# Expert weights in a two-layer MoE trunk: the limit on loads in flight is lifted, the room for them alone holds them back

## Chip, cores and metric

One core of one Trainium2 chip. Times are device microseconds of one execution. Before the change: 1047.03 us, median of three runs.

## What is computed

A trunk of two decoder layers over 512 tokens of width 1024, in float32. Layer 0 mixes tokens by RWKV-7 and gated linear attention, layer 1 by sparse attention. Each layer ends with the same kind of mixture of experts, which is what the change touches:

```
def _moe(h, router_w, router_bias, w_gate, w_up, w_down):
    s = jax.nn.sigmoid(hf @ router_w)
    ...                              # best of 4 groups of 4 experts, best 2 experts in it
    y = jnp.zeros(hf.shape, f32)
    for e in range(N_EXPERTS):       # 16
        he = (jax.nn.silu(hf @ w_gate[e]) * (hf @ w_up[e])) @ w_down[e]
        y = y + comb[:, e:e + 1] * he
    return y

h = _layer_norm(DN_ALPHA * x + mix, ln1_g[l], ln1_b[l])
ffn = _moe(h, ...)
x = _layer_norm(DN_ALPHA * h + ffn, ln2_g[l], ln2_b[l])
```

Gate and up are 1024 x 256 for each expert, down is 256 x 1024: 3.15 MB of float32 weights per expert, 50 MB per layer, and each is used once.

## The kernel before

Each layer is a mixer and then `moe_ln`. By the time of `moe_ln` the tokens' rows are stored in device memory as hD, and a copy of the residual as Y. `moe_ln` takes the 16 experts in order. A list of at most 128 tokens has been made for each expert (rtgt); what does not fit is left to a branch, `further`, which is not taken here, but where SP waits for all its DMAs to land.

For each expert the work is spread as follows. POOL issues a gather of the expert's rows, `fetch` (L974, `xg<-hD,rtgt`), two experts ahead. `turn` transposes them on PE (xtp, L986) and splits them into a high and a low part (xgh, xgl). `gate_up` loads four chunks of wgu, 128 x 1024 each, and multiplies; `hid_t` transposes the hidden values (htp, L1014); `down` loads two chunks of wdn, multiplies, copies the result to ys on ACT (L1035), and POOL issues a scatter (L1039, `Y<-ys,rtgt`) that adds it to Y. The last two experts add theirs on PE instead (zt, L1087), after Y has been read back (L1077, `hy<-Y`). There are two ys buffers. All scatters go to Y, so each one waits for the landing of the one before. In the order of one round the gate_up of expert e+1 comes before the down of expert e.

A weight chunk is loaded by SP (`Weights.part`, L566, 512 KB a load) into a raw buffer (named wr, room or hy after where its memory is), then ACT makes the rounded high part wh (L573) and DVE, or POOL for one chunk of an expert, the low part wl (L574). PE multiplies three times: high by high, low by high, high by low. The raw buffers of each layer's experts are a ring of 27, so a load may be issued when the chunk 27 loads earlier has been split. The two kinds of split outputs have nine pairs of buffers.

Two DMA queues carry all this: q1 holds what SP issues (loads, and the stores of hD and Y), q0 the gathers and scatters of POOL. Each works on all 16 DMA engines.

`Weights` is made in both layers with `flight` set to 3: a load also waits until the load three before it in program order has landed, whether or not there is room. The order of instructions on each engine is set by the scheduler of the framework; the loads stand in SP's queue in program order and are issued ahead of use as far as the ring and the limit allow, during the mixer for the first experts. The framework also gives SP's DMAs eight semaphore lanes in turn (DMAHW0 to DMAHW7); a DMA waits for the one before it in its own lane.

Of the kernel before, what the change touches and what calls it, by code (L numbers as in the profile page):

```python
# [66 lines left out]
def mm3(nc, out, ah, al, bh, bl, start, stop):  # L67
    nc.tensor.matmul(out, ah, bh, start=start, stop=False)  # L68
    nc.tensor.matmul(out, ah, bl, start=False, stop=False)  # L69
    return nc.tensor.matmul(out, al, bh, start=False, stop=stop)  # L70
# [890 lines left out]
def moe_ln(tc, k, I, L, w, xgp, xgs, tail, dbg):  # L961
# [3 lines left out]
    with ExitStack() as es:  # L965
# [5 lines left out]
        def fetch(e):  # L971

            xg = xgs[e % 3]
            nc.gpsimd.indirect_dma_start(out=xg, out_offset=None, in_=k.hD,  # L974
                                         in_offset=bass.IndirectOffsetOnAxis(ap=tgt[:, e:e + 1], axis=0),
                                         bounds_check=T - 1, oob_is_err=False)

        def turn(e):
            xg = xgs[e % 3]
            xh = xp.tile([P, KC, P], F32R, name="xgh", tag="xgh")  # L980
            xl = xp.tile([P, KC, P], F32R, name="xgl", tag="xgl")
            for hf in range(2):
                tp = k.ps.tile([P, 4, P], F32, name="xtp", tag="sm", bufs=3)
                for c in range(4):
                    cc = hf * 4 + c
                    nc.tensor.transpose(tp[:, c], xg[:, cc * P:(cc + 1) * P], k.ident)  # L986
                split_hi_lo(nc, xh[:, hf * 4:hf * 4 + 4], xl[:, hf * 4:hf * 4 + 4], tp)
            X[e] = xh, xl

        def chunk(e, j):  # L990
            return w.get(I["wgu"][L, e, :, j * 1024:(j + 1) * 1024], lo=nc.gpsimd if (j in LO0 if e == 0 else j == (1 if e > 13 else 3)) else None,
                         late=k.late if e < 2 else ())

        def gate_up(e):
            xh, xl = X.pop(e)
            gu = k.ps.tile([P, 512], F32, name="gu", tag="pj", bufs=2)
            for j in range(4):
                wh, wl = chunk(e, j)
                for c2 in range(2):
                    c = 2 * j + c2  # L1000
                    cs = slice(c2 * 512, c2 * 512 + 512)
                    mm3(nc, gu, xh[:, c], xl[:, c], wh[:, cs], wl[:, cs], c == 0, c == KC - 1)
            sg = hp.tile([P, 256], F32, name="sg", tag="sg")
            nc.scalar.activation(sg, gu[:, 0:256], AF.Sigmoid)
            tt(sg, gu[:, 0:256], sg, op=ALU.mult)
            hh = hp.tile([P, 256], F32, name="hh", tag="hh")
            stt(hh, sg, gate[:, e:e + 1], gu[:, 256:512], op0=ALU.mult, op1=ALU.mult)  # L1007
            H[e] = hh

        def hid_t(e):  # L1010
            hh = H.pop(e)
            tp = k.ps.tile([P, 2, P], F32, name="htp", tag="sm", bufs=3)
            for f in range(2):
                nc.tensor.transpose(tp[:, f], hh[:, f * P:(f + 1) * P], k.ident)  # L1014
            hth = hp.tile([P, 2, P], F32R, name="hth", tag="hth")
            htl = hp.tile([P, 2, P], F32R, name="htl", tag="htl")
            split_hi_lo(nc, hth, htl, tp)
            H[e] = hth, htl

        def down(e):  # L1020
            hth, htl = H.pop(e)
            wd = [w.get(I["wdn"][L, e, f], late=k.late if e < 2 else ()) for f in range(2)]
            if e >= 14:
                ys = w.pair()
            else:
                ys = yp.tile([P, D], F32, name="ys", tag="ys")
            for hf in range(2):
                cs = slice(hf * 512, hf * 512 + 512)
                yo = k.ps.tile([P, 512], F32, name="yo", tag="sv", bufs=2)
                for f in range(2):  # L1030
                    k.down = mm3(nc, yo, hth[:, f], htl[:, f], wd[f][0][:, cs], wd[f][1][:, cs], f == 0, f == 1)
                if e >= 14:
                    split_hi_lo(nc, ys[0][:, cs], ys[1][:, cs], yo)
                else:
                    nc.scalar.copy(ys[:, cs], yo)  # L1035
            if e >= 14:
                Y.append(ys)
                return
            nc.gpsimd.indirect_dma_start(out=k.Y, out_offset=bass.IndirectOffsetOnAxis(ap=tgt[:, e:e + 1], axis=0),  # L1039
                                         in_=ys, in_offset=None, bounds_check=T - 1, oob_is_err=False, compute_op=ALU.add)  # L1040
# [16 lines left out]
        for j, o in enumerate(onehot):  # L1057
            tt(o, k.iota[:, None, :].to_broadcast([P, NT, P]), dl[:, :, j:j + 1].to_broadcast([P, NT, P]), op=ALU.is_equal)
        gate_up(0)
        for e in range(16):  # L1060
            hid_t(e)
            if e + 2 < 16:
                fetch(e + 2)
                turn(e + 2)
            if e + 1 < 16:
                gate_up(e + 1)
            down(e)
# [328 lines left out]
def trunk(tc, ctx, k, I, out, dp, dbg):  # L1396
    nc = tc.nc
    with ExitStack() as es:
# [67 lines left out]
        with ExitStack() as ex:  # L1466
            with ExitStack() as e1:
# [46 lines left out]
                low = pool("wrawb", NRAW[1], elow)  # L1514
                w.rings(raws + [(low, NRAW[1])] + [k.h[:, i] for i in HSLOT[0]])
                moe_ln(tc, k, I, 0, w, xgp, xgs, lambda: elow.close() or x1_split(nc, k, lambda: pool("x1t", NT, ex)), dbg)
            if dbg:
                dbg("x1", k.h)
# [15 lines left out]
        with ExitStack() as e1:  # L1534
            right = lambda name, n: (pool(name, n, e1, side="right"), n)
            raws = [(few, 3)] + k.room + [right("wraw2", NRAW[2])]
            xgp = pool("xg1_", 1, e1, side="right")
            xgs = gather_bufs(xgp)
            for xg in xgs:
                nc.gpsimd.memset(xg, 0.0)  # L1540
            spl = right("wspl2", NSPL[1])[0]
            raws += [k.h[:, i] for i in HSLOT[1]] + [right("wraw3", NRAW[3]), right("wraw4", NRAW[4])]
            w = Weights(tc, raws, spl, FLIGHT)
            moe_ln(tc, k, I, 1, w, xgp, xgs, lambda: lambda i, x, cs=slice(0, D): nc.sync.dma_start(out[i * P:(i + 1) * P, cs], x[:, cs]), dbg)
# [109 lines left out]
```

## Time and profile before

| | before |
|---|---|
| median of three runs (lowest to highest) | 1047.03 us (1045.19 to 1048.56) |
| profiled execution | 1046.58 us |
| its span on the core | 1044.8 us |
| PE busy | 927.2 us, 89% |
| DVE busy | 781.9 us, 75% |
| ACT busy | 563.2 us, 54% |
| POOL busy | 318.0 us, 30% |
| q1 (SP's DMAs) | 158.02 MB, 45.2% of 16 engines |
| q0 (gathers, scatters) | 15.68 MB, 6.4% of 16 engines |

The experts of layer 0 run from about 425 to 600 us and those of layer 1 from about 855 to 1019 us of the span. Shares over the whole span mix these stages with the mixers, so the rows further down are taken from windows within them.

### The profile page before, as it was taken

What the parts mean: (1) busy time and instruction counts of PE and PEld (TensorE: products, weight loads), DVE (VectorE), ACT (ScalarE), POOL (GpSimd) and SP (SyncE); (2) the same over time, 40 slices, a digit from 0 to 9 for tenths busy, and PEclk for the clock granted to TensorE, in tenths of its full rate; (3) what the DMA queues carried; (4) which work ended last, traced back from release to release, by engine and by line L of the source; (5) the groups of instructions that cost most, each with busy time, mean ns of one, the idle gap of its engine ahead of it and who ended that gap; (6) DMA issues with size and microseconds to landing.
All of it is one profiled execution on the core that took longest, in us unless ns stands there. A gap on an engine that the chain in (4) does not pass through costs nothing. (4 is left out here: it accounts for less than half of the span.)

```text
span 1044.8 us, 14269 instructions
## 1 busy us (share of the span) xinstructions
PE 927.2 (89%) x4780; PEld 706.0 (68%) x4780; DVE 781.9 (75%) x1680; ACT 563.2 (54%) x912; POOL 318.0 (30%) x237
## 2 busy tenths in 40 slices
PE   7799988999998994899988689798999949999995
PEld 5577766776877783677776458675567737777773
DVE  4636689486587557799966678499993579989887
ACT  6435464334254213589867525154664238888872
POOL 2200212012021013375554131302400235665632
PEclk9999999999999997799999979898999959999998
DMA  6223103112106387798888745201414669889973
GB/s 222 94 66 100 51 1 91 36 57 67 35 6 228 120 284 262 256 285 271 261 268 262 250 170 161 82 1 61 141 41 165 238 215 306 281 276 301 285 248 144
DMA packets 72564, 174.72 MB, mean 167 GB/s; under 512 B 24595, under 2 KB 25907, under 8 KB 72480
## 3 DMA queue, kind: packets, MB, share of 16 engines
q1 hardware_dynamic: 63840, 158.02, 45.2%
q0 software_dynamic: 8640, 15.68, 6.4%
q8 instruction: 41, 0.67, 0.3%
q14 instruction: 43, 0.35, 0.1%
HBM read 163.23 MB, written 26.21 MB: 181 GB/s over the span
## 5 line engine op out<-in xcount | busy, mean ns | idle before, releaser
L574 DVE TENSOR_TENSOR wl<-wr,wh 128x1024 fp32r<-128x1024 f32 (+1 forms) x193 | 225.8, 1188 | 50.5 <-ACT wh L573 48.8
L573 ACT CAST wh<-wr 128x1024 fp32r<-128x1024 f32 (+2 forms) x233 | 219.4, 954 | 78.0 <-PE pj L69 29.8
L574 POOL TENSOR_TENSOR wl<-wr,wh 128x1024 fp32r<-128x1024 f32 (+2 forms) x40 | 103.5, 2592 | 167.5 <-ACT wh L573 103.7
L69 PE MATMUL gu<-wl,xgh 128*128 128x512 f32 x256 | 103.6, 405 | 0.9 <-DVE wl L574 0.8
L68 PE MATMUL gu<-wh,xgh 128*128 128x512 f32 x256 | 102.8, 402 | 0.0
L70 PE MATMUL gu<-wh,xgl 128*128 128x512 f32 x256 | 102.6, 401 | 0.0
L68 PE MATMUL pj<-xh,wh 128*128 128x512 f32 x208 | 86.2, 414 | 7.3 <-ACT xh L63 6.1
L70 PE MATMUL pj<-xh,wl 128*128 128x512 f32 x208 | 86.1, 414 | 0.0
L69 PE MATMUL pj<-xl,wh 128*128 128x512 f32 x208 | 85.6, 412 | 0.0
L1039 POOL DMA_INDIRECT Y<-ys,rtgt x28 | 58.5, 2091 | 62.9 <-ACT ys L1035 31.3
L974 POOL DMA_INDIRECT xg<-hD,rtgt x32 | 49.6, 1551 | 34.4 <-PE xtp L986 20.2
L69 PEld LDWEIGHTS gu<-wl,xgh 128*128 128x128 f32 x256 | 49.1, 192 | 14.2 <-POOL wl L574 2.4
L68 PEld LDWEIGHTS gu<-wh,xgh 128*128 128x128 f32 x256 | 49.1, 192 | 10.5 <-ACT xgh L63 0.6
L70 PEld LDWEIGHTS gu<-wh,xgl 128*128 128x128 f32 x256 | 49.0, 191 | 9.2
L69 PE MATMUL yo<-wl,hth 128*128 128x512 f32 x128 | 52.5, 410 | 2.5 <-DVE wl L574 2.4
L64 DVE TENSOR_TENSOR xgl<-xtp,xgh 128x512 fp32r<-128x512 f32 x64 | 41.1, 681 | 17.1 <-ACT xgh L63 12.3
L68 PE MATMUL yo<-wh,hth 128*128 128x512 f32 x128 | 50.8, 397 | 1.8 <-ACT hth L63 1.6
L68 PEld LDWEIGHTS pj<-xh,wh 128*128 128x128 f32 x208 | 39.8, 192 | 17.9 <-ACT xh L63 6.1
L70 PE MATMUL yo<-wh,htl 128*128 128x512 f32 x128 | 50.3, 393 | 0.0
L70 PE MATMUL pq<-wh,tl 128*128 128x512 f32 (+2 forms) x128 | 47.5, 371 | 0.0
L986 PE MATMUL xtp<-c_ident,xg 128*128 128x128 f32 x256 | 37.7, 296 | 10.7 <-DVEq L1045 5.7
L68 PE MATMUL pq<-wh,th 128*128 128x512 f32 (+2 forms) x128 | 46.6, 364 | 0.0
(422 smaller groups left out, 2215.0 us busy)
## 6 DMA issues: line engine op xcount, KB each, us to landing
wr<-in_wgu_dram SPq DMA_DIRECT2D x102, 512.0 KB, 6.5
wr<-in_wdn_dram SPq DMA_DIRECT2D x50, 512.0 KB, 7.2
wr<-in_w_dram SPq DMA_DIRECT2D x52, 256.0 KB, 2.7
wr<-in_wo_dram SPq DMA_DIRECT2D x16, 512.0 KB, 3.8
hy<-in_wgu_dram SPq DMA_DIRECT2D x15, 512.0 KB, 5.1
room<-in_wgu_dram SPq DMA_DIRECT2D x11, 512.0 KB
hy<-in_wdn_dram SPq DMA_DIRECT2D x9, 512.0 KB
hD<-hy SPq DMA_DIRECT2D x8, 512.0 KB, 2.7
```

What stands on the lines that cost most here:

```text
L64: nc.vector.tensor_tensor(lo, src, hi.bitcast(F32), op=ALU.subtract))
L68: nc.tensor.matmul(out, ah, bh, start=start, stop=False)
L69: nc.tensor.matmul(out, ah, bl, start=False, stop=False)
L70: return nc.tensor.matmul(out, al, bh, start=False, stop=stop)
L573: nc.scalar.copy(h[:, s], r[:, s])
L574: (lo or nc.vector).tensor_tensor(l[:, s], r[:, s], h[:, s].bitcast(F32), op=ALU.subtract)
L974: nc.gpsimd.indirect_dma_start(out=xg, out_offset=None, in_=k.hD, in_offset=bass.IndirectOffsetOnAxis(ap=tgt[:, e:e + 1], axis=0), bounds_ ...
L986: nc.tensor.transpose(tp[:, c], xg[:, cc * P:(cc + 1) * P], k.ident)
L1039: nc.gpsimd.indirect_dma_start(out=k.Y, out_offset=bass.IndirectOffsetOnAxis(ap=tgt[:, e:e + 1], axis=0), in_=ys, in_offset=None, bounds_c ...
```

## The change

After `gate_up(0)`, so after the program has written the loads of the first expert's four wgu chunks, `flight` is set to None. `part` then adds no wait to any later load of that layer: the first expert's wdn and all of experts 1 to 15. It happens in both layers. The object of a layer's experts is used for nothing behind them.

```
         gate_up(0)
+
+        w.flight = None
         for e in range(16):
             hid_t(e)
```

The lines that it acts on are these of `part`:

```
ld = nc.sync.dma_start(r[:, s], src[:, s])
if self.flight and len(self.loads) >= self.flight:
    behind(self.tc, ld, self.loads[-self.flight], wait=True)
```

On PE, DVE, ACT and POOL the order of instructions is the same. On SP the order is the same but for one load, and nearly every expert load has another wait. The first place is SP in the middle of layer 0's experts, six loads in a row (each row ends with the semaphores waited for: DMAHW is a lane of SP's DMAs, DVE, Activation and Pool the split that frees the raw buffer). Before:

```order
L566 DMA wr<-in_wgu_dram 128x1024 [waits DMAHW6_49,DVE_49]
L566 DMA wr<-in_wgu_dram 128x1024 [waits DMAHW7_49,DVE_49]
L566 DMA wr<-in_wgu_dram 128x1024 [waits DMAHW0_49,DVE_49]
L566 DMA wr<-in_wgu_dram 128x1024 [waits DMAHW1_49,DVE_49]
L566 DMA wr<-in_wdn_dram 128x1024 [waits DMAHW2_49,DVE_49]
L566 DMA wr<-in_wdn_dram 128x1024 [waits DMAHW3_49,DVE_49]
```

Each of these waits for the lane of the load three before it. The same six rows of SP in the changed kernel:

```order
L566 DMA wr<-in_wgu_dram 128x1024 [waits DMAHW1_49,DVE_49]
L566 DMA wr<-in_wgu_dram 128x1024 [waits DMAHW2_49,DVE_49]
L566 DMA wr<-in_wgu_dram 128x1024 [waits DMAHW3_49,DVE_49]
L566 DMA wr<-in_wgu_dram 128x1024 [waits DMAHW4_49,DVE_49]
L566 DMA wr<-in_wdn_dram 128x1024 [waits DMAHW5_49,DVE_49]
L566 DMA wr<-in_wdn_dram 128x1024 [waits DMAHW6_49,DVE_49]
```

The lane is now three further on, each load's own: it waits for the DMA eight before it, and for the room as before.

The second place is SP ahead of layer 1's experts, where the last rows of hD and Y are stored (the gathers read hD). Before:

```order
L566 DMA wr_9740<-in_wgu_dram 128x1024 [waits DMAHW2_49,PE_49]
L683 DMA hD_1387<-hy_64 128x1024 [waits Pool_49]
L683 DMA Y_1388<-hy_64 128x1024
L566 DMA hy_64<-in_wdn_dram 128x1024 [waits DMAHW4_49,DMAHW5_49,DMAHW0_49,DVE_49]
L683 DMA hD_1387<-hy_64 128x1024 [waits Pool_49]
L1650 BRANCH_PREFETCH_HINT
L683 DMA Y_1388<-hy_64 128x1024
L566 DMA wr_9752<-in_wgu_dram 128x1024 [waits DMAHW6_49,DMAHW1_49,PE_49]
L566 DMA hy_64<-in_wdn_dram 128x1024 [waits DMAHW7_49,DMAHW0_49,PE_49]
```

Here the load wr_9752 stands behind both pairs of stores. The same rows of SP in the changed kernel:

```order
L566 DMA wr_9740<-in_wgu_dram 128x1024 [waits DMAHW3_49,PE_49]
L566 DMA wr_9752<-in_wgu_dram 128x1024 [waits DMAHW4_49,PE_49]
L683 DMA hD_1387<-hy_64 128x1024 [waits DMAHW5_49,Pool_49]
L683 DMA Y_1388<-hy_64 128x1024
L566 DMA hy_64<-in_wdn_dram 128x1024 [waits DMAHW6_49,DMAHW5_49,DVE_49]
L683 DMA hD_1387<-hy_64 128x1024 [waits DMAHW0_49,Pool_49]
L1652 BRANCH_PREFETCH_HINT
L683 DMA Y_1388<-hy_64 128x1024 [waits DMAHW1_49]
L566 DMA hy_64<-in_wdn_dram 128x1024 [waits DMAHW1_49,DMAHW2_49,DMAHW0_49,PE_49]
```

The load wr_9752, which waits for PE to leave its buffer, has moved ahead of both pairs of stores, and the stores wait for lanes.

## Rows read from the trace of the kernel before

**Rows 1.** The page: its span, and one DMA queue (packets, MB, share of engines).

```profile
span 1044.8 us, 14269 instructions
...
q0 software_dynamic: 8640, 15.68, 6.4%
```

**Rows 2.** Windows: length, busy us (instructions) per engine, PE clock, DMA share, GB/s.

```profile
480.00:500.00 20.00, 19.52 (x96) 15.81 (x95) 18.31 (x22) 17.92 (x26) 13.28 (x7) 1.00 0.87 274
...
980.00:1000.00 20.00, 19.49 (x94) 15.16 (x93) 18.10 (x20) 17.43 (x25) 11.09 (x5) 1.00 0.89 283
```

**Rows 3.** SP's waits, 425 to 620, then 845 to 1030: total, times, longest.

```profile
SPq L566 <- DMA wr<-in_wgu_dram: 67.5, 37, 4.9
SPq L566 <- DMA wr<-in_wdn_dram: 35.1, 18, 5.4
...
SPq L566 <- POOL wl L574: 7.7, 3, 4.8
...
SPq L566 <- DMA wr<-in_wgu_dram: 63.0, 33, 4.8
```

**Rows 4.** ACT's waits from 425 to 620 us.

```profile
ACT wh L573 <- DMA wr<-in_wgu_dram: 12.7, 10, 3.8
```

**Rows 5.** Timeline of PE, layer 0: start, length, instruction, idle before and its releaser.

```profile
464.01 0.41 PE L1014 MATMUL htp<-c_ident,hh 128*128 128x128 f32 x2 [0.17 <-DVE hh L1007]
...
532.50 0.41 PE L1014 MATMUL htp<-c_ident,hh 128*128 128x128 f32 x2 [0.30 <-DVE hh L1007]
...
590.66 0.38 PE L1014 MATMUL htp<-c_ident,hh 128*128 128x128 f32 x2
```

**Rows 6.** Timeline of POOL, in layer 0 and from 925 in layer 1.

```profile
477.10 1.59 POOL L1039 DMA_INDIRECT Y<-ys,rtgt  x1 [1.60 <-ACT wh L573]
...
485.50 2.39 POOL L1039 DMA_INDIRECT Y<-ys,rtgt  x1 [0.16 <-ACT xgh L63]
...
492.69 2.38 POOL L574 TENSOR_TENSOR wl<-wr,wh 128x1024 fp32r<-128x1024 f32 x1 [2.69 <-issue]
...
585.30 1.93 POOL L1039 DMA_INDIRECT Y<-ys,rtgt  x1 [3.30 <-ACT hth L63]
...
925.25 2.27 POOL L1039 DMA_INDIRECT Y<-ys,rtgt  x1 [3.54 <-ACT ys L1035]
927.00 2.96 POOL L574 TENSOR_TENSOR wl<-wr,wh 128x1024 fp32r<-128x1024 f32 x1
...
935.51 2.27 POOL L1039 DMA_INDIRECT Y<-ys,rtgt  x1 [3.53 <-ACT ys L1035]
```

**Rows 7.** Issue to landing: scatters of 440-540, 860-980, at 477; gathers at 422, 426.

```profile
Y<-ys,rtgt POOLq DMA_INDIRECT x10, 9.2
...
Y<-ys,rtgt POOLq DMA_INDIRECT x11, 8.8
...
DMA to landing us min/median/max: 7.6/7.6/7.6
...
xg<-hD,rtgt POOLq DMA_INDIRECT x1, 4.3
...
xg<-hD,rtgt POOLq DMA_INDIRECT x1, 8.8
```

**Rows 8.** The page's costliest groups: busy, mean ns, idle before and its main releaser.

```profile
L69 PEld LDWEIGHTS gu<-wl,xgh 128*128 128x128 f32 x256 | 49.1, 192 | 14.2 <-POOL wl L574 2.4
```

**Rows 9.** Timelines of SP and, last row, PE at the end of layer 0's experts.

```profile
578.47 6.61 SPq L566 DMA_DIRECT2D wr<-in_wdn_dram  x4
...
596.58 1.75 SPq L1077 DMA_DIRECT2D hy<-Y  x4
...
600.00 2.05 PE L1087 MATMUL zt<-hy,c_ident 128*128 128x512 f32 x2 [4.36 <-DMA hy<-Y]
```

**Rows 10.** Timeline of SP ahead of layer 1's experts.

```profile
840.91 0.32 SPq L683 DMA_DIRECT2D hD<-hy  x1
...
842.76 0.38 SPq L566 DMA_DIRECT2D wr<-in_wgu_dram  x1
```

More of the change, by code (lines that the diff above doesn't have):

```diff
@@ L1059, in moe_ln @@
         gate_up(0)
+        w.flight = None
         for e in range(16):
```

## The prediction

> **What bounds the kernel now.** I read the page first, for the share of the span that each engine is busy and for the two DMA queues, then the windows of the two expert stages, then what SP, ACT and PE waited for there, and last the timelines of POOL and PE. The profiled execution has a span of 1044.8 us [rows 1] and took 1046.58 us, 0.45 under the median of 1047.03; the sum below is made against 1046.58. The change touches only the two expert stages, about 425 to 600 us (layer 0) and 855 to 1019 us (layer 1), and the loads that are issued ahead of them.
>
> In both stages PE is busy nearly all the time (19.5 of 20 us) and the DMA engines nearly so: share 0.87 at 274 GB/s in layer 0, 0.89 at 283 in layer 1 [rows 2]. SP spends most of its time on the limit that the change lifts. In layer 0 the waits of a load for an earlier load come to 67.5 + 35.1 us for the two largest kinds (126.9 with two smaller ones); waits for room are 7.7 us in one row. Layer 1 has 63.0 in its largest row [rows 3]. So the limit does bind, for half of each stage. Does anybody wait for the weights that come later because of it? In layer 0 yes, towards the end: ACT's cast of a fresh weight waits 12.7 us for loads of wgu [rows 4]. The rounds show it: the first transposes of two experts seven rounds apart stand at 464.01 and 532.50, so 9.78 us a round, and the next five rounds reach 590.66, 11.63 a round [rows 5]. Those five cost 58.16 − 5 x 9.78 = **9.2 us** too much. In layer 1 nobody waits for a weight: its rounds are 10.26 us from the first to the last full one, as the starts of the scatters at 925.25 and 935.51 show [rows 6], and among ACT's waits there the loads are next to nothing. What holds layer 1's round is another thing. POOL adds each expert's result to Y by a scatter, one after the other since all go to Y. A scatter lands 8.8 us (median) after its issue in layer 1 and 9.2 in layer 0 [rows 7], and the next is issued 0.8 us after that: the one issued at 477.10 landed after 7.6 us, at 484.7, and the next started at 485.50 [rows 6, 7]. A scatter and its 0.8 are 9.6 to 10 us: **as long as a round, in both layers**. In layer 1 the split of the last wgu chunk (wl, 927.00) stands right behind the scatter on POOL, and PE waits for it a little now (2.4 us over the kernel, [rows 8]); in layer 0 POOL does the scatter, the gather and then wl, with 2.69 us idle before wl [rows 6].
>
> **The change, part by part.** (1) The wait goes away, from every load of experts 1 to 15 in both layers; no instruction is added. What remains is the room (27 raw buffers) and the eight semaphore lanes over which SP's DMAs rotate: each load now waits for the DMA eight before it in place of the load three before it. So the limit is eight, not none.
>
> (2) The load queue fills. Six loads of 0.524 MB make 3.15 MB per expert; queue q0 moved 15.68 MB in about 30 gather and scatter pairs [rows 1], 0.52 MB each. A round needs 3.67 MB. By the windows a fully busy DMA moves 274/0.87 = 315 to 283/0.89 = 318 GB/s [rows 2], so a round is **11.6 us of DMA work**, against 9.78 and 10.26 of round. The limit of three hides this today: loads fall behind PE's use and eat the lead that they won before the stage. Without it SP has a backlog of up to eight loads until all weights are in, and the scatter and the gather must share the engines with it.
>
> (3) What the scatter then takes is not in the trace. Bounds: 7.6 us (the shortest one, less than now) and, if it stands behind five more loads of 0.524 MB/316 GB/s = 1.66 us, 8.8 + 8.3 = 17.1 us. The nearest rows: the gather issued at 422.74 with one load ahead landed in 4.3 us and one at 426.52 with three ahead in 8.8 [rows 7]; the scatter at 585.30 [rows 6], with the last of four loads and two vectors of 512 KB just ahead of it, was done for SP's next step at 596.58, 11.3 us later [rows 9]. So it grows with what SP has queued before it, by 1 to 2 us per transfer. I take it that it grows until the chain of scatters holds the rounds at the DMA's own 11.6 us, where the backlog stops growing (landing 10.8).
>
> By the Trainium skill, "DMA: Bandwidth & Descriptors", section "Queues, rings and completion order", each DMA engine takes turns between the queues that have work, a packet at a time; by that a deep queue of SP's would hold a scatter back no more than three loads do, which is the first rival below (1033.7 instead of 1056). The rows 7 and 9, where it took longer with more ahead, speak for order of arrival.
>
> (4) **Layer 1.** Room is for 27 loads, 4.5 rounds, so the last weight is loaded some 4 rounds before the end, and the backlog needs two or three rounds to build: 9 rounds at 11.6 − 10.26 = 1.34 give **+12.1**. Nothing is won against it: no weight was late.
>
> (5) **Layer 0.** 9 rounds at 11.6 − 9.78 = 1.82 give +16.4. Here a scatter may lag: POOL's idle 2.69 us a round and the second ys buffer let it fall behind between 2.7 us and a round of 9.8; I take 6, nearer the middle, so +10.4. The late weights of the last rounds come in time: −9.2. At the end PE waits 4.36 us for Y's rows, which wait for the last scatter [rows 9]; with no loads ahead of it, it lands in 7.6 and not 11.3: −3.7. Together **−2.5** (from −12.9, no delay, to +16.4, all of it and nothing won).
>
> (6) In layer 1 one load (the second wr load behind the two into hy) moves ahead of the last two stores of hD on SP's queue. Its buffer was free by 842.76, the last store of hD was issued at 840.91 [rows 10]: if PE frees it as late as that, stores and gathers come 1.9 us later, and behind its own 1.7 us of transfer at most 3.6 later. It may be free long before: I take 0. The waits on the limit ahead of the stages are few and lie beside the mixers' work: 0, between −1 and +2.
>
> **Sum:** 1046.58 + 12.1 − 2.5 = 1056.2; with the 0.45 to the median **1056.6 us**, 0.9% slower. Within this case the lag in layer 0 (2.7 to 9.8 us) and the count of rounds (7 to 11) give 1049 to 1068.
>
> **Rivals.** *Faster:* the scatter is not held back by a longer queue. Then layer 1 stays as it is and layer 0 gains 9.2 + 3.7 = 12.9: 1033.7 (1034.1 at the median). For it: 13% of the DMA's time in layer 0 is idle, 21 us of 160, and the landings now spread from 7.6 to 11.3 [rows 7, 9] without stopping PE in the middle; against it, [rows 7, 9] and a chain that is as long as the round already. It decides where landing plus 0.8 stays under 10.26. *Much slower:* the DMA's 0.87 is its ceiling with scatters in it, loads come no sooner, but the scatter stands behind them; then nothing is won in layer 0 and both layers stretch in full: 16.4 + 12.1 = +28.5, 1075. Against it: a share of 0.87 leaves 13% of the time in which the engines move no packet of either queue [rows 2], and a longer queue should fill it. *No change:* the chain absorbs a growing landing by its idle time and the late weights of layer 0 are paid for by layer 1, or a limit of eight acts as that of three did: 1047.
>
> **How the numbers follow.** Forecast (1049 to 1068, slower) 0.57; faster 0.24; no change 0.09; much slower 0.10. A difference under 0.3%, 3 us, could not be told from none. Faster 0.24, same 0.10 (0.01 from the forecast's lower end), slower 0.66. The range runs from 1033, the faster rival with half of what lies beyond it left out, to 1075. The forecast's own range is 1049 to 1068.
>
> **What would show it.** Right: SP's waits of loads for loads fall to a quarter, and waits for room and lanes take their place; median landing of scatters 10 to 12 us; layer 1's rounds near 11.6 through the middle and 9 to 10 in the last four; ACT's waits for wgu in layer 0 gone; DMA share over 0.95 until some 40 us before the end of each stage, then low. Wrong: landings at 9 us with the DMA at 0.95 and layer 1's rounds at 10.26 (the faster rival), or layer 0's last rounds still at 11 to 13 us with loads that are late (the slowest).

## The result: faster, and the profile after

The changed kernel took 1035.72 us (median of 16 runs, 1022.28 to 1049.77), the kernel before 1044.99 us (median of 16) in the same comparison: 9.3 us **faster** by the medians, a ratio of 0.991, where the forecast was 0.9% slower. The ratios with 95% intervals, here 0.9865 (0.9836 to 0.9894) or 14 us, leave out every run that is over 1.5% above the fastest of its kernel, here 8 of the 16 of the changed kernel and 1 of the 16 of the kernel before, so the gain is told as 9 to 14 us. A second comparison gave 0.991 (0.987 to 0.995), and 3.2 us, 0.997, by the medians of all its runs. The profiled execution took 1033.8 us with a span of 1032.0 (before: 1046.58 and 1044.8, [rows 1]). Single executions spread over 27 us (changed) and 16 us (before), so the stages are compared below, over several traces, not the spans of two.

Two windows of the expert stages of the changed kernel, with the columns of [rows 2]:

```profile
480.00:500.00 20.00, 19.51 (x96) 15.80 (x95) 18.31 (x21) 17.93 (x26) 11.77 (x7) 1.00 0.97 339
...
880.00:900.00 20.00, 18.97 (x91) 14.55 (x89) 17.78 (x21) 16.86 (x24) 12.37 (x6) 1.00 1.01 346
```

The DMA engines are full now: share 0.97 and 1.01, with 339 and 346 GB/s where [rows 2] had 0.87 at 274 and 0.89 at 283. (A packet counts in the window in which it starts, so a share can pass 1.) PE is as busy as before: 19.51 us against 19.52 in layer 0, and 18.97 in layer 1, where the kernel before has 18.98 from 900 to 920 us. So in these windows nothing was lost. SP's waits, 425 to 620 us, in the changed kernel:

```profile
SPq L566 <- DMA wr<-in_wgu_dram: 28.6, 18, 3.3
...
SPq L566 <- DVE wl L574: 19.6, 20, 2.3
SPq L566 <- POOL wl L574: 17.0, 8, 3.3
SPq L566 <- DMA wr<-in_wdn_dram: 16.0, 10, 3.2
```

The waits of loads for loads, 126.9 us before [rows 3], are 52.3 now with two smaller rows (these are the eight lanes), and the room, DVE's and POOL's wl, holds loads back for 36.6. ACT has no wait for an expert's weight left in layer 0. PE's timeline there, first transposes of experts:

```profile
498.10 0.41 PE L1014 MATMUL htp<-c_ident,hh 128*128 128x128 f32 x2 [0.31 <-DVE hh L1007]
...
527.40 0.41 PE L1014 MATMUL htp<-c_ident,hh 128*128 128x128 f32 x2 [0.19 <-DVE hh L1007]
...
538.29 0.41 PE L1014 MATMUL htp<-c_ident,hh 128*128 128x128 f32 x2 [1.24 <-DVE hh L1007]
...
584.67 0.38 PE L1014 MATMUL htp<-c_ident,hh 128*128 128x128 f32 x2
```

Three rounds from 498.10 to 527.40 are 9.77 us each, as before [rows 5]; one of 10.89 follows; and the five from 538.29 to 584.67 are 9.28 each where the last five before took 11.63. And the term on which the forecast rested, issue to landing of the scatters (minimum, median, maximum) from 480 to 550 us and from 900 to 965 in the changed kernel. The view knows the landings of three of the seven scatters in the first stretch and of three of the six in the second:

```profile
DMA to landing us min/median/max: 9.0/9.2/9.3
...
DMA to landing us min/median/max: 9.4/9.6/9.8
```

When each scatter is paired with the landings of its own semaphore in the trace, all seven have a median of 9.2 us (9.0 to 10.1) and all six one of 9.5 (9.2 to 9.8). In layer 0 this is the 9.2 of [rows 7], in layer 1 it is 0.7 above 8.8, with seven or eight loads outstanding in place of three. The loads from 480 to 550 us, paired in the same way, took 13.7 to 17.7 us, median 15.6 (36 loads), where they took 7.4 before (30 loads). When one of the seven scatters landed, two to four loads that had been issued ahead of it were still under way. **So a scatter lands before loads that were queued before it.** That settles the point on which forecast and faster rival parted. By the Trainium skill, "DMA: Bandwidth & Descriptors", section "Queues, rings and completion order", each DMA engine takes turns between the queues that have work; the trace agrees, with 9.2 us for the scatter beside 15.6 for the loads around it.

The end of layer 0's experts, PE in the changed kernel, against [rows 9]:

```profile
590.79 1.10 PE L1089 MATMUL zt<-hy,c_ident 128*128 128x512 f32 x2 [1.13 <-DMA hy<-Y]
```

PE waits 1.13 us there for Y's rows, not 4.36. And two such matmuls take 1.10 us, not 2.05. The windows just behind, of the changed kernel and then of the kernel before, show why (granted clock third from the right):

```profile
591.00:596.00 5.00, 5.00 (x18) 3.08 (x18) 2.13 (x6) 0.90 (x2) 0.00 (x0) 1.00 0.96 372
```

```profile
600.00:605.00 5.00, 5.00 (x9) 2.80 (x9) 0.70 (x1) 0.00 (x0) 0.00 (x0) 0.50 1.02 409
```

After its long wait PE ran at 0.50, 1.2 GHz, before the change: 9 instructions in 5 us. Now it stays at 1.00, 2.4 GHz: 18.

### The profile page after: what moved, and what is told of

Same layout as the page of the kernel before. It is cut to its first block, busy times and chain, and to the rows that moved or that the text cites. A ratio compares the mean times of both kernels' runs of the same rounds, so it can differ in the third digit from the quotient of the medians.

```text
span 1032.0 us, 14251 instructions
## 1 busy us (share of the span) xinstructions
PE 920.4 (89%) x4780; PEld 702.4 (68%) x4780; DVE 789.3 (76%) x1680; ACT 564.7 (55%) x912; POOL 315.9 (31%) x237
## 4 chain that ended last, share of the span: by engine, by line
PE 45%; DVE 32%; DMA 11%; issue 6%; ACT 5%; POOL 1%; DVEq 0%; SPq 0%; POOLq 0%; ACTq 0%
DVE wl L574 9%; PE pj L69 3%; PE pj L68 3%; PE pj L70 3%; DMA wr<-in_wgu_dram 3%; PE po L70 3%; PE po L69 2%; ACT wh L573 2%; DVE room L1319 2%; PE po L68 2%; DVE m L1318 2%; DMA Y<-ys,rtgt 2%; DMA xg<-hD,rtgt 2%; PE zt L1089 2%; PE gu L70 2%
## 5 line engine op out<-in xcount | busy, mean ns | idle before, releaser
L574 DVE TENSOR_TENSOR wl<-wr,wh 128x1024 fp32r<-128x1024 f32 (+1 forms) x193 | 232.9, 1226 | 37.6 <-ACT wh L573 36.1
L574 POOL TENSOR_TENSOR wl<-wr,wh 128x1024 fp32r<-128x1024 f32 (+2 forms) x40 | 105.8, 2650 | 133.7 <-ACT wh L573 57.5
L1039 POOL DMA_INDIRECT Y<-ys,rtgt x28 | 55.8, 1994 | 90.7 <-ACT ys L1035 25.2
L64 DVE TENSOR_TENSOR xgl<-xtp,xgh 128x512 fp32r<-128x512 f32 x64 | 41.3, 680 | 17.7 <-ACT xgh L63 16.4
L68 PEld LDWEIGHTS pj<-xh,wh 128*128 128x128 f32 x208 | 39.9, 192 | 17.9 <-ACT xh L63 6.3
```

Of the source, the lines that this page charges most:

```text
L64: nc.vector.tensor_tensor(lo, src, hi.bitcast(F32), op=ALU.subtract))
L574: (lo or nc.vector).tensor_tensor(l[:, s], r[:, s], h[:, s].bitcast(F32), op=ALU.subtract)
```

## The experiments

Each kernel has one trace here, and all times of stages below are worked out from these: "rounds" is the sum of the 15 gaps between the first transposes (htp) of the 16 experts, "end" the time from the last of these in layer 0 to the first transposes of the next layer (x1tp), which holds the read-back of Y and the layer norm.

| kernel | limit, layer 0 / 1 | rounds, layer 0 | end, layer 0 | rounds, layer 1 |
|---|---|---|---|---|
| before | 3 / 3 | 154.4 | 25.5 | 147.5 |
| before, again (e8) | 3 / 3 | 149.3 | 25.2 | 147.5 |
| e2 | 3 / none | 148.3 | 23.5 | 147.9 |
| changed | none / none | 143.8 | 16.9 | 147.7 |
| changed, again (e11) | none / none | 142.1 | 16.2 | 147.9 |
| e1 | none / 3 | 148.8 | 18.0 | 147.5 |
| e3 | 5 / 5 | 148.4 | 18.0 | 147.6 |
| e4 | 2 / 2 | 176.9 | 20.7 | 182.8 |
| e5, no scatters | none / none | 142.2 | 18.0 | 147.4 |
| e6 | 3, none from expert 4 on | 152.1 | 18.0 | 147.9 |
| e7, wl on DVE, experts 1 to 13 | none / none | 144.7 | 15.5 | 143.2 |
| e9, wl on DVE, all | none / none | 138.5 | 24.6 | 139.2 |
| e10, wl on DVE, all | 3 / 3 | 152.2 | 17.9 | 152.7 |

**Which layer gains.** My theory after the result (theory A) was the faster rival: a scatter is not held back by a longer queue, so layer 1 stays as it is and layer 0 gives the whole gain. Its rival (B) was that layer 1 has a share in it. The limit was lifted in one layer at a time.

```
-        w.flight = None
+        if L == 0:                  # e2: if L == 1
+            w.flight = None
```

> The limit is lifted in layer 0 alone. Theory A (the scatter does not stand behind the longer queue of loads; the gain is layer 0's late weights and its end): all of the gain, ratio 0.985 to 0.99 to the kernel before, layer 0's rounds 9.7 to 9.9 us to the last, scatters landing in a median of 9.2 us with eight loads outstanding; layer 1 as before, 10.27 us a round. Theory B (layer 1 has a share in the gain, by an earlier start of its experts): half of it, 0.992 to 0.995.

> The limit is lifted in layer 1 alone. Theory A: nothing, ratio 0.997 to 1.003, layer 1's rounds at 10.27 us, its scatters landing 0.2 to 0.5 us later than with the limit. Theory B: 0.992 to 0.995. My forecast, that the chain of scatters stretches the rounds of layer 1, would show here alone, as 1.008 to 1.012.

Layer 0 alone: 0.9951 (0.9907 to 0.9996), 1037.66 us. Layer 1 alone: 0.9979 (0.9950 to 1.0008), 1040.50 us. Layer 1 alone cannot be told from no change, and is not the 1.008 that my forecast's mechanism would have given; its rounds take 147.9 us with the limit off and 147.5 with it on. In layer 0 the gain is there, but smaller than the 0.985 to 0.99 expected, and its rounds were not all at 9.8: three late ones took 10.8, 10.9 and 12.4 us. The two ratios together make 0.7%, less than the 1.35% and 0.9% that the same kind of ratio gave in the two comparisons of the whole change; their intervals leave room for both, and what layer 1 adds, if anything, stays open.

**How the landing goes with depth.** The limit was set to five and to two.

```
-        w.flight = None
+        w.flight = 5                # e4: 2
```

> A limit of five in place of none, in both layers. Theory A: the scatter's landing does not depend on the depth beyond three or four loads, 9.0 to 9.6 us as with eight; the DMA is near full already, so most of the gain is there, 0.985 to 0.992. Order of arrival: landing lies between that of three and of none, and grows by 1.3 to 1.7 us for each load, to 12 us; then layer 1's rounds would be 12.5 us.

> A limit of two, in both layers. Theory A: fewer loads at the engines than their turns can fill, so that the scatter lands sooner, 7.5 to 8.5 us, and the loads come slower: over 2.8 us a load in place of 2.4, so that layer 0's weights are late from round 5 or 6 on; 30 to 60 us slower than before. Order of arrival: landing 1.3 to 1.7 us less than with three, 7.3 to 7.7 us. The runs with three, five and none against this one give the curve of the landing over the depth.

Scatters from 480 to 550 us, with a limit of five and then with a limit of two:

```profile
DMA to landing us min/median/max: 8.8/9.1/10.0
```

```profile
DMA to landing us min/median/max: 9.3/9.5/9.7
```

These views know three of six landings and two of six. With every scatter paired as above, the medians for two, three, five and eight loads outstanding are 9.2, 9.4, 10.0 and 9.2 us in this stretch, and 8.8, 8.8, 9.4 and 9.5 from 900 to 965 us. Single scatters spread from 6.2 to 10.4 us at two and from 9.0 to 10.1 at eight. So from two loads to eight the median moves by less than 1 us, where the order of arrival had asked for 1.3 to 1.7 us for each load, and even at two it is not the 7.3 to 8.5 that both theories had expected. With no load outstanding it is shorter: the last two scatters of layer 0 in the changed kernel landed in 6.9 and 6.7 us. For a scatter in these stages it counts that loads are there, and hardly how many. Five in flight gave 0.9915 (0.9885 to 0.9945), 1034.98 us, as good as none within the intervals. Two in flight took 1103.21 us in its one run, 61 us more than the kernel before beside it: DMA share 0.77 in the window from 540 to 560, ACT waiting 28.5 us for wgu from 500 to 640, and rounds of mostly 14.4 to 17.0 us late in both stages. So the limit has to be high enough to fill the engines, and beyond that it does not matter here.

**Does the chain of scatters set a round?** The scatters were left out; the results of experts 0 to 13 are then missing from Y.

```
-            nc.gpsimd.indirect_dma_start(out=k.Y, out_offset=..., in_=ys, ..., compute_op=ALU.add)
```

> The changed kernel without the scatters of experts 0 to 13 (their results are left out of Y, the rest is computed). It asks whether the chain of scatters sets any round. My prediction held that it is as long as a round in both layers: then layer 1's rounds fall from 10.27 to 9.8 us or less without it. Theory A with the chain just off the path: layer 1 stays at 10.27; in layer 0 the rounds of 10.8 to 12.4 us that three runs show late in the stage, where POOL's and DVE's wl fall together, are gone, all at 9.7 to 9.85.

First transposes in layer 1 without scatters:

```profile
899.94 0.41 PE L1014 MATMUL htp<-c_ident,hh 128*128 128x128 f32 x2 [0.51 <-DVE hh L1007]
910.33 0.41 PE L1014 MATMUL htp<-c_ident,hh 128*128 128x128 f32 x2 [0.52 <-DVE hh L1007]
920.72 0.41 PE L1014 MATMUL htp<-c_ident,hh 128*128 128x128 f32 x2 [0.50 <-DVE hh L1007]
```

10.39 us a round, where it was 10.27 with them: **the scatters do not set layer 1's round**, though their chain is nearly as long. In layer 0 all rounds from the third to the twelfth are at 9.73 to 9.84. That fits odd rounds of 10.8 us and more that come from the scatters, but it does not show it: this is one trace, and e11, with all its scatters, has no odd round either.

How such a round comes about is seen in the changed kernel. An ordinary round at 517 us, POOL and then DVE:

```profile
516.98 2.41 POOL L574 TENSOR_TENSOR wl<-wr,wh 128x1024 fp32r<-128x1024 f32 x1 [0.41 <-issue]
```

```profile
518.30 2.16 DVE L574 TENSOR_TENSOR wl<-wr,wh 128x1024 fp32r<-128x1024 f32 x1 [0.78 <-ACT wh L573]
```

The next one, at 528 us, again POOL and then DVE:

```profile
526.05 1.72 POOL L974 DMA_INDIRECT xg<-hD,rtgt  x1 [0.32 <-DMA hy<-in_wgu_dram]
527.79 2.42 POOL L574 TENSOR_TENSOR wl<-wr,wh 128x1024 fp32r<-128x1024 f32 x1
```

```profile
528.15 3.15 DVE L574 TENSOR_TENSOR wl<-wr,wh 128x1024 fp32r<-128x1024 f32 x1 [0.90 <-ACT wh L573]
531.23 0.41 DVE L64 TENSOR_TENSOR htl<-htp,hth 128x256 fp32r<-128x256 f32 x1
```

A scatter and the 0.8 to the next make 10.0 us, the round 9.78, so the chain falls behind by some 0.2 us a round; POOL's gather and wl stand behind the scatter and fall behind with it. POOL's wl lies on one of DVE's in every round, but by more now: DVE's started 1.32 us after POOL's at 517 us and took 2.16, and starts 0.36 us after it at 528 and takes 3.15, where one alone takes 1.2. This is the round of 10.89. In both pairs of rows DVE's wl ends 1.1 us after POOL's, and so it is with all 30 in the expert stages of the changed kernel that begin while POOL's runs: they end 1.08 to 1.09 us after it, however early they began. So DVE's does not go on more slowly beside POOL's; it makes next to no progress until POOL's is done.

**What does set layer 1's round.** There too POOL's wl lies on DVE's in every round. With the scatters it stands right behind one [rows 6]; in the changed kernel, POOL and then DVE:

```profile
935.85 2.98 POOL L574 TENSOR_TENSOR wl<-wr,wh 128x1024 fp32r<-128x1024 f32 x1
```

```profile
937.65 2.28 DVE L574 TENSOR_TENSOR wl<-wr,wh 128x1024 fp32r<-128x1024 f32 x1
```

Without them (e5) the two still overlap, POOL's from 912.92 to 915.36 us and DVE's from 914.05 to 916.45. So POOL's share of this work was given to DVE, in e7 for experts 1 to 13, in e9 for all.

```
-lo=nc.gpsimd if (j in LO0 if e == 0 else j == (1 if e > 13 else 3)) else None
+lo=nc.gpsimd if (j in LO0 if e == 0 else e > 13 and j == 1) else None     # e9: lo=None
```

> The changed kernel with the low parts of experts 1 to 13 all made by DVE (POOL made every fourth wgu chunk's). Where POOL's and DVE's wl fall together, DVE's takes 2.1 to 3.2 us in place of 1.2. If this is what sets layer 1's 10.27 us and layer 0's odd rounds of 10.8 us, layer 1's rounds fall to 9.8 us, 4 to 5 us for the kernel, and the scatter is issued 0.8 us after the landing before. If DVE has no room for the 1.2 us a round more, rounds grow by up to 1.2 us, 10 to 25 us slower.

> The changed kernel with every low part made by DVE, those of the last two experts too. In the run before it the rounds were 9.34 us, but PE waited 3.3 to 3.7 us in each layer for POOL's wl of expert 14, which stood behind scatters that lag. If that is all, these rounds (14.8 and 16.8 us) become 9.4 to 11 us, and the kernel is 6 to 12 us faster than that run: 1014 to 1020 us. If the lag of the scatters then stops ACT at the two ys buffers instead, half of that is lost: 1020 to 1024.

First transposes of layer 1 in e7:

```profile
866.19 0.38 PE L1014 MATMUL htp<-c_ident,hh 128*128 128x128 f32 x2
875.53 0.38 PE L1014 MATMUL htp<-c_ident,hh 128*128 128x128 f32 x2
884.87 0.38 PE L1014 MATMUL htp<-c_ident,hh 128*128 128x128 f32 x2
```

9.34 us a round, in both layers, with DVE busy 19.7 of 20 us: further down than expected, and it was POOL's wl that set the round. Whether by holding up DVE's or by being late itself is not separated, as e7 took away both; for POOL's late wl alone PE had waited only 2.6 us in 11 rounds of the changed kernel. But now the chain of scatters is longer than a round by 1.0 us (scatters start 10.3 us apart), and falls behind to the end. PE's waits at the end of layer 0's experts, in e7:

```profile
PE gu L69 <- POOL wl L574: 3.7, 1, 3.7
```

That is POOL's wl of expert 14 behind late scatters, a round of 16.8 us. In e9, where DVE makes it, the lag shows as these waits of ACT and PE in layer 0:

```profile
ACT ys L1035 <- DMA Y<-ys,rtgt: 3.2, 3, 1.4
```

```profile
PE zt L1089 <- DMA hy<-Y: 4.8, 1, 4.8
```

The two ys buffers stop ACT, and PE waits 4.8 us for the last scatter, with the low clock behind it. e7 took 1025.83 us (0.9842, 0.9765 to 0.9919), e9 1030.25 (0.9912, 0.9882 to 0.9942), so e9's 1014 to 1024 was missed: it moved the wait and did not remove it. Whether e7 beats the change cannot be told from these intervals; its four runs, 1022.6 to 1029.5, lie at the fast end of the change's.

> The kernel before, limit of three kept, with every low part made by DVE. If loads of 2.2 to 2.4 us each are the bound behind it, rounds of 9.34 us use up the lead sooner, and both layers wait for weights: 6 x 2.2 = 13 us a round at the end, layer 1 too, for the first time; 1035 to 1050 us. If the limit does not matter with shorter rounds, 1022 to 1028.

e10 is e9's edit on the kernel before, with the limit of three: 1041.15 us, 0.9988 (0.9959 to 1.0018). The same rounds of 9.34 us come first; then, but for the last, they take 10.8 to 13.8 us in both layers. ACT's wait for weights in layer 1 of e10, where no limit-3 kernel above had one:

```profile
ACT wh L573 <- DMA wr<-in_wgu_dram: 11.0, 7, 2.9
```

So what the limit costs depends on the round: at 10.27 us nothing, at 9.78 the last rounds of layer 0, at 9.34 both layers.

**The first gathers.** The limit was kept for the loads ahead of the first gathers and the branch.

```
-        w.flight = None
         for e in range(16):
+            if e == 4:
+                w.flight = None
```

> The limit of three stays until the loads for expert 4 are written (those that stand ahead of the first gathers and the branch) and is lifted from there on, in both layers. Theory A: the first two gathers of layer 0 land in 6.6 us as before the change, not in 9.4 to 9.7, and PE begins the stage 1 to 2.5 us sooner against the gather's issue; all else as in the changed kernel: 0 to 2.5 us faster than that, ratio to the kernel before 0.984 to 0.992. If the early loads matter more than the gathers, rounds late in layer 0 wait for weights again.

0.9877 (0.9832 to 0.9922), 1030.32 us: the same as the change within the interval, and one or two microseconds are below what these times can tell. Its traced execution was the slowest of its ten, 1041.56 us. There the first two gathers landed in 6.4 and 7.3 us, as expected; late rounds of 11.1 to 12.5 us came back in layer 0, but not by weights, for which ACT does not wait there, and their cause stays open. The cost at the gathers is seen in the other traces. The first two gathers of layer 0, issue to landing, in the kernel before again (e8) and in the changed kernel again (e11, where the view knows one of the two):

```profile
DMA to landing us min/median/max: 7.4/7.5/7.6
```

```profile
DMA to landing us min/median/max: 9.6/9.6/9.6
```

From the first gather's issue to the first htp it is 22.3 to 22.9 us in the three traces with the limit in layer 0 (before, e2, e8), 23.8 to 24.8 in three without (changed, e1, e11): 1.6 us lost at the start. Here the landing does grow with the limit, paired as above: 5.1 and 7.7 us with two in flight, 6.6 and 6.6 with three (before), 8.4 and 9.1 with five, 9.4 and 9.7 in the changed kernel. Why these gathers do and the scatters of the stages hardly do stays open.

**The two kernels again.**

> The kernel before, once more, for its trace: how much layer 0's late weights cost in another execution. In the first trace 15 rounds took 154.4 us, in the run with layer 1's limit alone lifted 148.3. Theory A expects 147 to 155, and over 9.9 us a round from the 10th on; the changed kernel had 143.8.

> The changed kernel once more, beside the two above and for a second trace: 1030 to 1040 us, 0.984 to 0.992 of the kernel before; layer 0's 15 rounds in 143 to 149 us (143.8 in its first trace, 148.8 with the limit lifted in layer 0 alone), by how often POOL's and DVE's wl fall together.

e8 took 1045.03 us, e11 1038.27 (0.991, 0.987 to 0.995). Layer 0's rounds take 149.3 us in e8: by the prediction's own reckoning the late weights cost 4 us there, 9 in its trace. In e11 they take 142.1, with no odd round at all.

## Why the prediction was wrong

**The step that failed is (3)**, the growth of the scatter's landing with what SP has queued. It took 10.8 us, between 7.6 and 17.1, and measured 9.2 in layer 0 and 9.5 in layer 1; from two loads outstanding to eight the medians lie between 8.8 and 10.0. The rows that it rested on were misread. The two gathers of [rows 7] differ in whether loads shared the engines for long, 4.3 us with one load nearly done and 8.8 with three, and not in how many were ahead; 8.8 is about what a scatter takes beside any number of loads from two to eight, and I drew a line through it. The gather between the two, at 424.03, was not looked at: it had no load outstanding ahead of it and three issued 0.7 to 1.4 us behind it, and took 9.4 us (paired as above), longer than the one with three ahead. The scatter of 585.30 [rows 6, 9] took 11.2 us, and the same scatter took 11.3 in e8 and 10.5 in e2, so it is no chance value; but it had four loads and vectors outstanding, while scatters with seven or eight took 8.8 to 10.8. What lengthens it stays open. With 15.6 us for a load and 9.2 for a scatter issued behind it, order of arrival is excluded.

**(1) was right:** no instruction, and a limit of eight lanes; SP still waits 52.3 us for loads, so that it is not the room alone, as the title has it, that holds them back. **(2) was right in kind, wrong in size:** the engines fill, to 0.97 to 1.01, but then move 339 to 346 GB/s; dividing GB/s by the share had given 316. A round's 3.67 MB are then 10.7 us of DMA work and not 11.6, so that even a chain bound to it would have cost a third of the forecast in layer 1 (10.7 − 10.26) and half in layer 0 (10.7 − 9.78).

**(4), layer 1, +12.1 us, was wrong:** rounds 147.5 in all three traces with the limit (before, e8, e1), 147.7 to 147.9 in three without (changed, e11, e2), so +0.3. Two premises fell: the landing grew by 0.7 us only, and the round was not the chain of scatters. That a chain is as long as a round does not say that it sets the round; e5 took it away and the round did not fall. POOL's wl set it (e7). What comes behind layer 1's last htp took 29.9 us in place of 30.5 in the same traces, −0.6, which the sum did not have.

**(5), layer 0, −2.5 us.** Its three parts, as means of three traces with the limit (before, e8, e2: rounds 150.7, end 24.7) and three without (changed, e11, e1: 144.9 and 17.0). The rounds alone just overlap, 148.3 at the least with the limit and 148.8 at the most without; rounds and end together do not, 171.8 to 179.9 and 158.3 to 166.8:
- The late weights, −9.2, and the stretch by the scatters, +10.4, lie both in the rounds: −5.8 together. Against 142.2 without scatters the limit costs 8.5, so the first was about right as a mean (12.3, 7.1 and 6.2 in the three), and read from one execution that was the worst of three. The stretch is 0 to 6.6 us in the three, 2.7 in the mean, by the odd rounds, if they do come from scatters that lag: then the forecast's mechanism exists, at a quarter of its size.
- The end, −3.7, measured −7.7. PE's wait for Y fell by 3.6 (4.1 to 0.5), as forecast. The 36 matmuls that add Y and the last experts took 2.4 us less (13.3 to 10.9), as the low clock in them went with the wait; the sum had left this out. The last 1.6 are a wait of 2.3 us of PE for DVE ahead of the next layer's first transposes, which all three traces with the limit have and one of the three without (e1); its cause stays open.

**(6)** The load that moved ahead of the stores in layer 1 cost nothing: the last store of hD and the first gather stand 4.1 us apart in both traces (840.91 [rows 10] and 845.02 before; 828.83 and 832.90 after). The loads ahead of layer 0's stage cost 1.6 us at the first gathers, inside the −1 to +2 given.

The sum as measured: +1.6 − 5.8 − 7.7 + 0.3 − 0.6 = −12.2 us, between the 9 and 14 us of the first comparison. The faster rival had the mechanism, and its 1033.7 is near the profiled 1033.8, partly by luck: it left out the start and the clock, and the two profiled executions also differ by some 6 us in the mixers, where nothing was changed. It had 0.24, and the text named what would show it, landings at 9 us with the DMA at 0.95 and rounds at 10.26; that is what came. I gave it too little because I took two landings for a law.

## What to carry to other kernels

Before a longer queue of loads is priced as a delay for another queue, look for a pair in the trace where a late transfer on the one lands ahead of an early one on the other, and compare landings at several depths; a single long landing shows nothing. A chain as long as the round is not yet what sets it: take it away in a run and see whether the round moves. A limit on loads in flight costs nothing while the lead lasts and whole microseconds a round once it is used up, so its price is read from the last rounds of a stage, and over several executions.

## What was not expected of the hardware

- A scatter on q0 landed in 8.8 to 10.0 us (medians of the two stretches) with two, three, five or eight loads outstanding on q1, and in 6.7 to 6.9 with none, while a load of 512 KB went from 7.4 us at three in flight to 15.6 at eight.
- A tensor_tensor on DVE that began while one ran on POOL took 1.7 to 3.3 us in place of 1.2 (30 in the changed kernel), and ended 1.08 to 1.09 us after POOL's each time. The Trainium skill, "VectorE: DVE Perf Modes", section "Two Vector instructions with no wait between them", states that an operation with two inputs in SBUF reads one of them through an interface that it shares with GpSimd; the lengthened wl is such an operation, and e7, which took POOL's away, brought the round from 10.27 to 9.34 us.
- A wait of 4.4 us before the matmuls that add Y cost 2.9 us more behind it, as they ran at 0.50 of the clock at first: two of them took 2.05 us in place of 1.10, and all 36 from there to the next layer took 13.9 in place of 11.0.
